# Decoder trunk with stick-breaking attention: another hand-written order for the attention stage and the output projection behind it

## The chip, the cores and the metric

The kernel runs on one core of one Trainium2 chip. The metric is the device time of one execution in microseconds (us); lower is better. The kernel before took 908.56 us (median of three runs, 906.37 to 910.4).

## The reference

The input is one sequence of 512 tokens with 1,024 channels, in fp32. There are two layers, each followed by a squared-ReLU MLP with 4,096 hidden channels, and every sublayer has an RMSNorm before and one behind. The first layer is a pooling mixer. The second is attention with 16 heads of 64 channels; its keys and values come from one projection of the residual stream. What matters here is the second layer's attention, and the projection of its result:

```python
q = jnp.matmul(h, w_q[j])                      # k, v come from w_kv in the same way
z = q_blk @ k_blk.T * inv_sqrt_d               # scores, strictly causal
log1m = jnp.where(mask, -softplus(z), 0.0)
excl = cumsum(log1m, reverse=True) - log1m
a = jnp.where(mask, exp(log_sigmoid(z) + excl), 0.0)
o = a @ v
m = jnp.matmul(o, w_o[j])                      # output projection
x = x + rms_norm(m, mix_post_g)                # norm behind; then a norm ahead of the MLP
```

## The kernel before, in words

**Precision.** Every fp32 product is made of three matmuls: both operands are split into a rounded high part and the rest, the low part, and high times high, high times low and low times high are added up in one PSUM bank. PSUM has 8 banks of 512 columns here, handed out in turn, so a product that needs a bank waits until an earlier one is read.

**Pairs.** Attention goes pair of heads by pair of heads, eight pairs. Of a pair `p` there are, by the letters of the order table:
- `J` and `Q`: the projections of its keys and queries (`project`, `up_block`, L836 to L838, 24 matmuls of 512 columns each). `j` and `q` cast the result out of its bank: ACT writes the high part (L1167, L1168, L1181), DVE the low part (L1170, L1183).
- `S`: the scores, 16 matmuls of up to 512 columns (L1210), into six banks. `G`: ACT's sigmoids, which read them (L1234, L1238).
- `X` and `M`, for each of the two heads: DVE's scan over a row (L1243) and the product with the sigmoid (L1334).
- `T`, for each head: 10 transposes on PE into three banks (L1259) and three copies by ACT (L1261).
- `A`: attention times values, 16 matmuls (L1269); `a`: the split of the result, ACT the high part (L414), DVE the low part (L415).

PE works one pair ahead: between `S` of pair p and `S` of pair p+1 stand `J` and `Q` of p+1, then `A` of p-1 and `T` of p.

**Values.** `V` and `v` are the seven products of the value projection (L1120, 24 matmuls each) and what reads their banks (L1136); `F` makes operands for them. Most lie ahead of the first pair; `V4` and `V6` stand beside pair 0 and pair 1.

**Weights.** Most weights were split earlier in the program and stored in DRAM; SP loads them back as two transfers of 512 KB, high and low (L361, source `kept`), in the order of a queue, each as soon as a slot of its ring is free. The last ones are split during attention itself, in the order of the list `LATE`: the two halves of `V6`'s weight, keys and queries of pairs 4 to 7, the output weights `o0` to `o7` and four weights of the MLP behind. Each goes through `L`, the load of the raw weight by SP (L223; four buffers, `raw` twice, `spare`, `late`); `g`, for keys and queries only, DVE's multiply by the norm's gain (L230); `W`, ACT's cast to the high part (L249; L252 for `V6`); `w`, DVE's subtraction that leaves the low part (L258; L261 for `V6`). `s` stores a split weight to DRAM for later (L203).

SP's queue holds both kinds of loads and takes them one after the other: a load whose buffer is not yet free holds up all loads behind it.

**Output projection.** `Z` is `out_product` for one tile of 128 tokens: `Z034` adds pairs 3 and 4 to tile 0, both halves of 512 columns, three matmuls for each pair and half (L455 to L457). The table does pairs 0 to 6 of tiles 0 and 1; behind the table the last pair follows, and then tiles 2 and 3 whole, half by half. Behind each tile come the squares' sum (L418), the norm of the sum (L507), the norm ahead of the MLP (L532), and the transposes of the normed tile (`transpose`, L541, 8 each), which are read out as `xnh` and `xnl` (L414, L415). The MLP's first products on tiles 0 and 1 need the first two tiles' transposes.

**What sets the order.** In this stage every engine runs its instructions in the order in which the program issues them: PE, ACT, DVE, POOL and SP follow the table `ATT_ORDER` letter by letter, each taking from it what is its own. The loop behind it reads

```python
        with tc.manual_schedule(engines={on.PE, on.Activation, on.DVE, on.Pool, on.SP}):
            for what, i, a in ATT_ORDER:
```

`fill()` in it (behind `J`, `Q`, `V` and the early `W`) issues the next loads of stored weights, as far as the ring has room.

Of the kernel before, what the change touches and what calls it, by code (L numbers as in the profile page):

```python
# [28 lines left out]
PAIRS = HEADS // 2  # L29
# [25 lines left out]
ATT_ORDER = [  # L55
    (w[0], int(w[1:2] or 0), int(w[2:] or 0))
    for w in """V5 N2 v5 V0 N3 V3 F3 v0 J0 v3 F2 j0 Q0 L L L L q0 V1 v1 F1 V2 v2
    S0 G0 X00 M00 J1 W X01 w L V4 M01 j1 T00 T01 W F4 v4 w L Q1 q1 V6 v6 g
    S1 G1 g X10 M10 X11 J2 M11 W j2 w L Q2 W q2 w L A0 a0 T10 T11
    S2 G2 g X20 M20 X21 J3 M21 W j3 w L g Q3 q3 W w L A1 a1 T20 T21  # L60
    S3 G3 g X30 M30 X31 J4 M31 W j4 w L Q4 g q4 A2 a2 T30 T31
    S4 G4 g X40 M40 X41 J5 M41 W j5 w L Q5 W q5 w L A3 a3 T40 T41
    S5 G5 g X50 M50 X51 J6 M51 W j6 w L Q6 W q6 w L A4 a4 T50 T51
    S6 G6 X60 M60 X61 J7 M61 W j7 w L Q7 W q7 w L A5 a5 T60 W w L T61
    S7 A6 G7 X70 Z002 M70 W X71 w Z102 M71 W T70 w R a6 W w L W Z034 Z134 w L W T71 w L Z055 Z155
    W w L A7 W w Z066 Z166 a7 W w s""".split()
]


# [21 lines left out]
def trunk(ctx, tc, x, consts, gcol, grow, pw, wup, wdn, wq, wk, wv, wo, out):  # L91
# [14 lines left out]
    def ps():  # L106
        return psum.tile([P, 512], F32, tag="ps", name=name("ps"))
# [257 lines left out]
    def fill(n=1):  # L365
        if gate[0]:
            behind.update(latest)
        for _ in range(n):
            if queue and sum(map(in_ring, made)) < ahead and (queue[0][0][0] != "dn" or dn_pool[0]):
                if not any(x["key"] == queue[0][0] for x in late) or queue[0][0] in kept:  # L370
                    make()

    def get(key):
        while key not in made:
            make()
        return made.pop(key)
# [68 lines left out]
    def by_twos(w, cut):  # L445

        if len(w.shape) == 3:
            half = w[:, 4 * (cut.start // 512) :][:, : KC // 2]
            return half.rearrange("p (j b) c -> p b c j", j=2)
        half = w[:, NS[cut.start // 512]].rearrange("p (j i) -> p i j", j=2)  # L450
        lo = cut.start % 512 // 2
        return half[:, lo : lo + (cut.stop - cut.start) // 2]

    def mm3(dst, ah, al, bh, bl, start, stop):
        nc.tensor.matmul(dst, ah, bh, start=start, stop=False)  # L455
        nc.tensor.matmul(dst, ah, bl, start=False, stop=False)  # L456
        nc.tensor.matmul(dst, al, bh, start=False, stop=stop)  # L457
# [599 lines left out]
    with tc.tile_pool(name="att", bufs=1, reuse_waits="tile") as ap:  # L1057
# [40 lines left out]
        def value_product(i):  # L1098
            key = VALUES[i][1]
            w = [get(("v", i, h)) for h in range(2)]  # L1100
            banks = [None, None]
            linked = i in (0, 2, 4, 6)
            for t in range(2):
                if key in left:
                    a = [[x[:, q, TS[t]] for q in range(4)] for x in left[key]]
                else:
                    n, k = int(key[0]) - 1, int(key[1]) - 1
                    need(2 * n + t)
                    a = [[x[:, 4 * k + q, TS[2 * n + t]] for q in range(4)] for x in (xnh, xnl)]
                if not linked:  # L1110
                    bank = ps()
                elif i == 0:
                    bank = ps()
                    chain.append(bank)
                else:
                    bank = chain[t]
                for q in range(4):
                    cols = NS[q % 2]
                    for n, (x, z) in enumerate(((0, 0), (0, 1), (1, 0))):
                        nc.tensor.matmul(  # L1120
                            bank, a[x][q], in_turn(w[q // 2][z][:, cols], 512),
                            start=(i == 0 or not linked) and q == 0 and n == 0, stop=q == 3 and n == 2,
                            skip_group_check=True,
                        )

                banks[t] = bank
            fill()
            results[i] = banks
# [155 lines left out]
        def out_product(t, cs, halves=range(2)):  # L1284
            for n in halves:
                if (t, n) not in sums:
                    sums[t, n] = ps()
                for c in cs:
                    if c not in wos:
                        wos[c] = get(("o", c))  # L1290
                    (lh, ll), (wh, wl) = os[c], wos[c]
                    mm3(
                        sums[t, n], lh[:, TS[t]], ll[:, TS[t]], by_twos(wh, NS[n]), by_twos(wl, NS[n]),
                        c == 0, c == PAIRS - 1,
                    )
# [4 lines left out]
        with tc.manual_schedule(engines={on.PE, on.Activation, on.DVE, on.Pool, on.SP}):  # L1300
            for what, i, a in ATT_ORDER:
                if what == "V":
                    value_product(i)
                elif what == "v":
                    value_out(i)
                elif what == "F":
                    form(i)
                elif what == "W":
                    late_high()
                    if upto["W"] < 16:  # L1310
                        fill()
                elif what in "Lgws":
                    {"L": late_load, "g": late_scale, "w": late_low, "s": late_store}[what]()
                elif what == "R":
                    gpost1, gpre1 = gain_row(R_MIX_POST1), gain_row(R_MLP_PRE1, spare_tile())
                elif what == "N":
                    need(i)
                elif what in "JQ":
                    project(("k" if what == "J" else "q", i))
                    fill()  # L1320
                elif what == "j":
                    keys(i)
                elif what == "q":
                    queries(i)
                elif what == "S":
                    pzs[i] = scores((qs[i], ks[i]))
                elif what == "G":
                    for a in range(2):
                        ws[i, a] = sigmoids(pzs[i], a)
                elif what == "X":  # L1330
                    es[i, a] = scanned(a)
                elif what == "M":
                    w = ws[i, a]
                    latest["dve"] = nc.vector.tensor_tensor(out=w, in0=w, in1=es.pop((i, a)), op=ALU.mult)  # L1334
                elif what == "T":
                    parts[i, a] = transposed(ws.pop((i, a)))
                elif what == "A":
                    mix_pair(i)
                elif what == "a":
                    mixed_out(i)  # L1340
                elif what == "Z":
                    out_product(i, range(a // 10, a % 10 + 1))
            assert upto["W"] == upto["w"] == len(late) and not going, upto
            ups = [Update(t, gpost1, None, gpre=gpre1) for t in range(T)]

            def evacuate(t, n):
                up, bank = ups[t], sums.pop((t, n))
                up.halves = (up.halves or []) + [ap.tile([P, 512], F32, tag="at", bufs=6, name=name("at"))]
                up.just_square(n, bank)
                latest["dve"] = nc.vector.tensor_tensor(  # L1350
                    out=up.halves[n], in0=bank, in1=gpost1[:, NS[n]], op=ALU.mult
                )

            for t in range(2):
                for n in range(2):
                    out_product(t, [PAIRS - 1], [n])
                    evacuate(t, n)
                ups[t].factor()
            for t in range(2):
                ups[t].sums_added()  # L1360
                ups[t].rstd()
            for t in range(2):
                ups[t].norm()
            out_product(2, range(PAIRS), [0])
            evacuate(2, 0)
            out_product(2, range(PAIRS), [1])
            ups[0].transpose()
            evacuate(2, 1)
            ups[2].factor()
            out_product(3, range(PAIRS), [0])  # L1370
            ups[2].sums_added()
            ups[1].transpose()
            evacuate(3, 0)
            ups[2].rstd()
            ups[2].norm()
            out_product(3, range(PAIRS), [1])
            fill(4)
            evacuate(3, 1)
            ups[3].factor()
            ups[3].sums_added()  # L1380
            ups[3].rstd()
            ups[3].norm()
            pending.update({t: ups[t] for t in (T - 2, T - 1)})
# [68 lines left out]
```

## Time and profile before

The profiled execution took 908.8 us. Its span, from the first to the last instruction, is 907.0 us, so 1.8 us lie around it. TensorE's granted clock was 0.996 of full speed over the span.

| what | before |
|---|---|
| median of three runs | 908.56 us (906.37 to 910.4) |
| profiled execution, its span | 908.8 us, 907.0 us |
| PE busy | 891.8 us, 98% of the span |
| DVE busy, ACT busy | 700.7 us (77%), 541.2 us (60%) |
| scores of pair 1 (`S1`) start at | 421.23 us |
| first products of the last MLP (L836, 256 columns) start at | 584.02 us |

The trace's lines give the start in us from the span's start, the duration, the engine, the program line, the operation, the tiles written and read, the count, and in brackets the engine's idle time ahead with what ended it. `SPq` is SP's queue of DMA instructions; its duration covers the time for which the instruction was held, not the transfer.

### The profile page before, as it was taken

To read this page: it belongs to the slowest core of one execution; us is meant where nothing else is said; L and a number is where in the kernel's file an instruction comes from. 1 tells how busy PE (TensorE), PEld (TensorE's weight loads), DVE (VectorE), ACT (ScalarE), POOL (GpSimd) and SP (SyncE) were. 2 spreads that over 40 slices of the span, in tenths; PEclk is the share of its full clock that TensorE was granted. 3 is DMA by queue.
4 is the path that set the end of the run, shared out by engine and by line. 5 is a ranking of instruction groups with operands and counts; after the bars stand their busy time and mean duration, and the time that the engine had idled before them with its cause. 6 is when DMAs were issued, how large, how long until landed. Compare 5 with 4: busy or idle time off the path is not lost.

```text
span 907.0 us, 11746 instructions
## 1 busy us (share of the span) xinstructions
PE 891.8 (98%) x4522; PEld 771.0 (85%) x4522; DVE 700.7 (77%) x716; ACT 541.2 (60%) x880; POOL 86.5 (10%) x82
## 2 busy tenths in 40 slices
PE   9999999999999999999999999999999999999997
PEld 7998888888888888878778877898888888888886
DVE  5956799996988976776988884665596876967956
ACT  6757747476796847364778864456554454544632
POOL 2100000000000014000000000111120310403103
PEclk9999999999999999999999999999999999999999
DMA  7443558277696732955121126232504233133102
GB/s 282 172 184 138 177 186 287 114 262 265 241 353 251 268 126 77 383 198 225 47 70 47 47 70 231 79 131 98 205 24 159 96 139 117 47 139 116 45 27 93
DMA packets 39150, 141.01 MB, mean 155 GB/s; under 512 B 3968, under 2 KB 4442, under 8 KB 39094
## 3 DMA queue, kind: packets, MB, share of 16 engines
q1 hardware_dynamic: 38946, 140.24, 42.5%
q8 instruction: 36, 0.59, 0.3%
q14 instruction: 20, 0.16, 0.0%
q10 hardware_dynamic: 148, 0.02, 0.0%
HBM read 116.12 MB, written 24.12 MB: 155 GB/s over the span
## 4 chain that ended last, share of the span: by engine, by line
PE 79%; DVE 7%; ACT 5%; DMA 5%; issue 2%; SPq 0%; POOL 0%; POOLq 0%; DVEq 0%; ACTq 0%
PE ps L723 24%; PE ps L836 13%; PE ps L838 13%; PE ps L837 12%; PE ps L1120 3%; PE ps L455 2%; DMA xn<-in_wdn 2%; PE ps L456 2%; PE ps L457 2%; DMA w<-kept 2%; PE ps L975 2%; PE ps L1210 2%; PE ps L1269 1%; PE ps L951 1%; DMA raw<-in_wup 1%
## 5 line engine op out<-in xcount | busy, mean ns | idle before, releaser
L723 PE MATMUL ps<-w,a 128*128 128x512 f32 x1176 | 267.0, 379 | 0.7 <-ACT a L414 0.7
L836 PE MATMUL ps<-xnh,w 128*128 128x512 f32 (+1 forms) x704 | 254.2, 362 | 2.4 <-DMA w<-kept 2.3
L838 PE MATMUL ps<-xnh,w 128*128 128x512 f32 (+1 forms) x704 | 253.9, 361 | 0.1
L837 PE MATMUL ps<-xnl,w 128*128 128x512 f32 (+1 forms) x704 | 253.8, 361 | 0.0
L723 PEld LDWEIGHTS ps<-w,a 128*128 128x128 f32 x1176 | 221.8, 189 | 33.6 <-ACT a L414 1.5
L836 PEld LDWEIGHTS ps<-xnh,w 128*128 128x128 f32 x704 | 133.2, 190 | 18.0 <-ACT w L252 2.6
L838 PEld LDWEIGHTS ps<-xnh,w 128*128 128x128 f32 x704 | 133.8, 190 | 16.4 <-DMA w<-kept 0.8
L837 PEld LDWEIGHTS ps<-xnl,w 128*128 128x128 f32 x704 | 133.8, 190 | 15.4
L154 DVE TENSOR_TENSOR w<-raw,w 128x1024 fp32r<-128x1024 f32 x56 | 69.3, 1239 | 53.4 <-ACT w L152 53.4
L152 ACT CAST w<-raw 128x1024 fp32r<-128x1024 f32 x56 | 58.5, 1045 | 76.0 <-PE ps L838 75.4
L732 DVE TENSOR_TENSOR y<-ps,y 128x512 f32<-128x512 f32 x124 | 82.7, 682 | 19.6 <-PE ps L723 19.6
L414 ACT CAST w<-e 128x1536 fp32r<-128x1536 f32 (+1 forms) x30 | 41.7, 1391 | 47.3 <-DVE e L696 33.7
L414 ACT CAST a<-r 128x768 fp32r<-128x768 f32 (+1 forms) x60 | 47.0, 785 | 35.3 <-DVE r L677 23.0
L415 DVE TENSOR_TENSOR w<-e,w 128x1536 fp32r<-128x1536 f32 (+1 forms) x30 | 53.9, 1797 | 9.9 <-ACT w L414 9.7
L415 DVE TENSOR_TENSOR a<-r,a 128x768 fp32r<-128x768 f32 (+1 forms) x60 | 60.1, 1002 | 0.6 <-ACT a L414 0.6
L1243 DVE TENSOR_TENSOR_SCAN e<-u,begin 128x1280 f32<-128x1280 f32 x16 | 45.2, 2825 | 17.7 <-ACT u L1234 16.9
L485 POOL TENSOR_TENSOR y<-y,grow 128x512 f32<-128x512 f32 x8 | 12.4, 1546 | 341.8 <-ACT xn L418 341.8
L415 DVE TENSOR_TENSOR w<-xn,w 128x1536 fp32r<-128x1536 f32 (+1 forms) x20 | 33.0, 1651 | 9.4 <-ACT w L414 9.1
L414 ACT CAST w<-xn 128x1536 fp32r<-128x1536 f32 (+1 forms) x20 | 27.8, 1389 | 17.9 <-PE ps L723 17.9
L755 ACT ACTIVATE r<-ps 128x512 f32<-128x512 f32 x56 | 33.0, 590 | 8.6 <-PE ps L838 8.6
L415 DVE TENSOR_TENSOR w<-w,w 128x1536 fp32r<-128x1536 f32 (+1 forms) x20 | 32.9, 1646 | 6.7 <-ACT w L414 6.6
L414 ACT CAST w<-w 128x1536 fp32r<-128x1536 f32 (+1 forms) x20 | 27.9, 1393 | 16.1 <-PE ps L723 15.8
(189 smaller groups left out, 1269.5 us busy)
## 6 DMA issues: line engine op xcount, KB each, us to landing
raw<-in_wup SPq DMA_DIRECT2D x63, 512.0 KB, 4.3
w<-kept SPq DMA_DIRECT2D x42, 512.0 KB, 5.9
w<-in_wdn SPq DMA_DIRECT2D x8, 1536.0 KB, 6.0
xn<-in_wdn SPq DMA_DIRECT2D x8, 1536.0 KB, 8.1
kept<-wx SPq DMA_DIRECT2D x20, 512.0 KB, 5.1
kept<-apart SPq DMA_DIRECT2D x16, 512.0 KB, 6.1
apart<-in_wv SPq DMA_DIRECT2D x10, 512.0 KB, 5.2
raw<-in_wdn SPq DMA_DIRECT2D x8, 512.0 KB, 4.8
```

The costliest lines, as they stand in the source:

```text
L152: nc.scalar.copy(hi, raw)
L154: nc.vector.tensor_tensor(out=lo, in0=raw, in1=hi.bitcast(F32), op=ALU.subtract)
L414: latest["act"] = nc.scalar.copy(hi, src)
L415: latest["dve"] = nc.vector.tensor_tensor(out=lo, in0=src, in1=hi.bitcast(F32), op=ALU.subtract)
L723: nc.tensor.matmul(bank, a[:, x, q, TS[t]], by_twos(w[:, z, q], NS[0]), start=start and q == 0 and k == 0, stop=q == self.n - 1 and k == 2 ...
L732: nc.vector.tensor_tensor(out=part, in0=bank, in1=part, op=ALU.add)
L755: nc.scalar.activation(split_up(r, 256), in_order(pu, 256), ACT.Relu)
L836: nc.tensor.matmul(pu[:, cols], wh[:, k, :], xh, start=k == 0, stop=False)
L837: nc.tensor.matmul(pu[:, cols], wh[:, k, :], xl, start=False, stop=False)
L838: nc.tensor.matmul(pu[:, cols], wl[:, k, :], xh, start=False, stop=k == KC - 1)
L1120: nc.tensor.matmul(bank, a[x][q], in_turn(w[q // 2][z][:, cols], 512), start=(i == 0 or not linked) and q == 0 and n == 0, stop=q == 3 and ...
L1243: nc.vector.tensor_tensor_scan(out=e[:, ::-1], data0=us[a][:, 1:][:, ::-1], data1=begin[:, ::-1], initial=0.0, op0=ALU.mult, op1=ALU.max,)
```

## The change

The table `ATT_ORDER` is rewritten from pair 0 on; `z206` is new, a `Z` for one half only (tile 2, pairs 0 to 6, first half); and the code behind the table puts the transposes of tiles 0 and 1 later. Every engine has as many instructions as before (PE 3114, DVE 678, ACT 735, SP 214 rows of the program, the same kinds).

```diff
@@ ATT_ORDER @@
-    S0 G0 X00 M00 J1 W X01 w L V4 M01 j1 T00 T01 W F4 v4 w L Q1 q1 V6 v6 g
-    S1 G1 g X10 M10 X11 J2 M11 W j2 w L Q2 W q2 w L A0 a0 T10 T11
-    S2 G2 g X20 M20 X21 J3 M21 W j3 w L g Q3 q3 W w L A1 a1 T20 T21
-    S3 G3 g X30 M30 X31 J4 M31 W j4 w L Q4 g q4 A2 a2 T30 T31
-    S4 G4 g X40 M40 X41 J5 M41 W j5 w L Q5 W q5 w L A3 a3 T40 T41
-    S5 G5 g X50 M50 X51 J6 M51 W j6 w L Q6 W q6 w L A4 a4 T50 T51
-    S6 G6 X60 M60 X61 J7 M61 W j7 w L Q7 W q7 w L A5 a5 T60 W w L T61
-    S7 A6 G7 X70 Z002 M70 W X71 w Z102 M71 W T70 w R a6 W w L W Z034 Z134 w L W T71 w L Z055 Z155
-    W w L A7 W w Z066 Z166 a7 W w s""".split()
+    S0 G0 X00 M00 J1 W X01 w V4 M01 j1 T00 T01 W F4 v4 w Q1 q1 V6 v6
+    S1 G1 g g X10 M10 X11 J2 L L M11 W j2 w Q2 q2 A0 a0 T10 T11 W
+    S2 G2 w g X20 M20 X21 J3 M21 W j3 w L L Q3 q3 g A1 a1 T20 T21 W
+    S3 G3 w g X30 M30 X31 J4 M31 W j4 w L L Q4 q4 g A2 a2 T30 T31 W
+    S4 G4 w g X40 M40 X41 J5 M41 W j5 w L L Q5 q5 g A3 a3 T40 T41 W
+    S5 G5 w L L X50 M50 X51 J6 M51 W j6 w L Q6 q6 A4 a4 T50 T51 W
+    S6 G6 w X60 M60 X61 J7 M61 W j7 w L L L Q7 q7 A5 a5 T60 T61 W
+    S7 A6 G7 w L X70 Z002 M70 W X71 w Z102 M71 W T70 w R a6 W w L W Z034 Z134 w L W T71 w L Z055 Z155
+    W w L A7 W w Z066 Z166 z206 a7 W w s""".split()
@@ the loop @@
-                elif what == "Z":
-                    out_product(i, range(a // 10, a % 10 + 1))
+                elif what in "Zz":
+                    out_product(i, range(a // 10, a % 10 + 1), range(2) if what == "Z" else [0])
@@ behind the table @@
-            out_product(2, range(PAIRS), [0])
+            out_product(2, [PAIRS - 1], [0])
             evacuate(2, 0)
             out_product(2, range(PAIRS), [1])
-            ups[0].transpose()
             evacuate(2, 1)
             ups[2].factor()
             out_product(3, range(PAIRS), [0])
             ups[2].sums_added()
-            ups[1].transpose()
+            ups[0].transpose()
             evacuate(3, 0)
             ups[2].rstd()
+            out_product(3, range(PAIRS // 2), [1])
+            ups[1].transpose()
             ups[2].norm()
-            out_product(3, range(PAIRS), [1])
+            out_product(3, range(PAIRS // 2, PAIRS), [1])
             fill(4)
```

**SP's queue around the loads of Q1, J2, Q2, J3 and Q3** (the stored weights, L361, each as high and low) and the raw loads of the late weights (L223):

```order
 L361 DMA w_3353<-kept_1481 128x1024 x2
-L223 DMA raw_3360<-in_wk 128x1024
-L361 DMA w_3386<-kept_2357 128x1024 x2
-L361 DMA w_3438<-kept_2403 128x1024 x2
-L223 DMA raw_3451<-in_wq 128x1024
-L361 DMA w_3478<-kept_2480 128x1024 x2
+L361 DMA w_3384<-kept_2357 128x1024 x2
+L361 DMA w_3436<-kept_2403 128x1024 x2
+L361 DMA w_3474<-kept_2480 128x1024 x2
+L361 DMA w_3506<-kept_2554 128x1024 x2
+L361 DMA w_3584<-kept_2619 128x1024 x2
+L223 DMA raw_3587<-in_wk 128x1024
+L223 DMA raw_3589<-in_wq 128x1024
```

`kept_2357` is Q1's weight. Two raw loads (`k5` and `q5` of `LATE`) stood one ahead of it and one behind the next; now both stand behind five loads of stored weights.

**DVE from the keys of pair 3 to the first scan of pair 3.** Before:

```order
L1170 TENSOR_TENSOR kl_2960<-ps_3736,k_3764 64x512 x2
L258 TENSOR_TENSOR w_3762<-raw_3360,w_3762 128x1024
L230 TENSOR_TENSOR raw_3451<-raw_3451,gc 128x1024
L1183 TENSOR_TENSOR q_3800<-ps_3775,q_3800 64x512 x2
L258 TENSOR_TENSOR w_3805<-raw_3451,w_3805 128x1024
L415 TENSOR_TENSOR ohl_3819<-ps_3810,ohl_3819 128x512
L230 TENSOR_TENSOR spare_3602<-spare_3602,gc 128x1024
L1243 SCALAR_TENSOR_TENSOR e_3902<-u_2963,begin 128x1280
```

and now:

```order
L1170 TENSOR_TENSOR kl_2960<-ps_3732,k_3760 64x512 x2
L258 TENSOR_TENSOR w_3758<-raw_3587,w_3758 128x1024
L1183 TENSOR_TENSOR q_3797<-ps_3772,q_3797 64x512 x2
L230 TENSOR_TENSOR raw_3589<-raw_3589,gc 128x1024
L415 TENSOR_TENSOR ohl_3812<-ps_3803,ohl_3812 128x512
L258 TENSOR_TENSOR w_3853<-raw_3589,w_3853 128x1024
L230 TENSOR_TENSOR spare_3768<-spare_3768,gc 128x1024
L1243 SCALAR_TENSOR_TENSOR e_3898<-u_2963,begin 128x1280
```

The queries' low part (L1183) stands one instruction earlier, ahead of the scaling of the next weight; the second subtraction (L258) stands behind the split of the attention's result. On ACT, at the same place, the cast that this subtraction needs (L249) stood ahead of that split and of the six copies of the transposes; now it stands behind the copies, ahead of the sigmoids of the next pair.

**PE behind the table's last `Z`** (`ohl_4665` is the split result of pair 6, `ohl_4770` before and `ohl_4792` now that of pair 7, `ohl_3641` that of pair 0; `ps_4593` is a sum of tile 0, `ps_4770` now the first half of tile 2). Before, and now:

```order
L457 MATMUL ps_4628<-w_4674,ohl_4665 128x512
L455 MATMUL ps_4593<-h_4754,ohl_4770 128x512
L456 MATMUL ps_4593<-l_4755,ohl_4770 128x512
L457 MATMUL ps_4593<-h_4754,ohl_4770 128x512
L455 MATMUL ps_4603<-h_4754,ohl_4770 128x512
```

```order
L457 MATMUL ps_4628<-w_4674,ohl_4665 128x512
L455 MATMUL ps_4770<-w_4272,ohl_3641 128x512
L456 MATMUL ps_4770<-w_4273,ohl_3641 128x512
L457 MATMUL ps_4770<-w_4272,ohl_3641 128x512
L455 MATMUL ps_4770<-w_4365,ohl_3812 128x512
...
L457 MATMUL ps_4770<-w_4674,ohl_4665 128x512
L455 MATMUL ps_4593<-h_4754,ohl_4792 128x512
```

Between the last matmul on pair 6 and the first on pair 7 now lie the 21 matmuls of `z206`. The transposes of tile 0 (L541) stood behind 48 matmuls of tile 2; now they stand behind the first half of tile 3, and those of tile 1 in the middle of its second half.

More of the change, by code (lines that the diff above doesn't have):

```diff
@@ L57 @@
     for w in """V5 N2 v5 V0 N3 V3 F3 v0 J0 v3 F2 j0 Q0 L L L L q0 V1 v1 F1 V2 v2
-    S0 G0 X00 M00 J1 W X01 w L V4 M01 j1 T00 T01 W F4 v4 w L Q1 q1 V6 v6 g
-    S1 G1 g X10 M10 X11 J2 M11 W j2 w L Q2 W q2 w L A0 a0 T10 T11
-    S2 G2 g X20 M20 X21 J3 M21 W j3 w L g Q3 q3 W w L A1 a1 T20 T21
-    S3 G3 g X30 M30 X31 J4 M31 W j4 w L Q4 g q4 A2 a2 T30 T31
-    S4 G4 g X40 M40 X41 J5 M41 W j5 w L Q5 W q5 w L A3 a3 T40 T41
-    S5 G5 g X50 M50 X51 J6 M51 W j6 w L Q6 W q6 w L A4 a4 T50 T51
-    S6 G6 X60 M60 X61 J7 M61 W j7 w L Q7 W q7 w L A5 a5 T60 W w L T61
-    S7 A6 G7 X70 Z002 M70 W X71 w Z102 M71 W T70 w R a6 W w L W Z034 Z134 w L W T71 w L Z055 Z155
-    W w L A7 W w Z066 Z166 a7 W w s""".split()
+    S0 G0 X00 M00 J1 W X01 w V4 M01 j1 T00 T01 W F4 v4 w Q1 q1 V6 v6
+    S1 G1 g g X10 M10 X11 J2 L L M11 W j2 w Q2 q2 A0 a0 T10 T11 W
+    S2 G2 w g X20 M20 X21 J3 M21 W j3 w L L Q3 q3 g A1 a1 T20 T21 W
+    S3 G3 w g X30 M30 X31 J4 M31 W j4 w L L Q4 q4 g A2 a2 T30 T31 W
+    S4 G4 w g X40 M40 X41 J5 M41 W j5 w L Q5 q5 g A3 a3 T40 T41 W
+    S5 G5 w L L X50 M50 X51 J6 M51 W j6 w L Q6 q6 A4 a4 T50 T51 W
+    S6 G6 w X60 M60 X61 J7 M61 W j7 w L L L Q7 q7 A5 a5 T60 T61 W
+    S7 A6 G7 w L X70 Z002 M70 W X71 w Z102 M71 W T70 w R a6 W w L W Z034 Z134 w L W T71 w L Z055 Z155
+    W w L A7 W w Z066 Z166 z206 a7 W w s""".split()
 ]
```

## The prediction

> **What bounds the kernel now.** First the page's line of busy time, then the table of PE's waits in the stage that is reordered (370 to 600 us), then the timeline around each of them.
>
> ```profile
> PE 891.8 (98%) x4522; PEld 771.0 (85%) x4522; DVE 700.7 (77%) x716; ACT 541.2 (60%) x880; POOL 86.5 (10%) x82
> ```
>
> ```profile
> PE ps L836 <- DMA w<-kept: 2.3, 1, 2.3
> PE ps L1210 <- ACT at L1261: 1.0, 2, 0.8
> PE ps L541 <- DVE xn L532: 0.6, 1, 0.6
> PE ps L1210 <- DVE q L1183: 0.5, 1, 0.5
> PE ps L1210 <- DVE ohl L415: 0.4, 2, 0.2
> PE ps L455 <- ACT ohl L414: 0.4, 1, 0.4
> ```
>
> PE is the bound, and the change leaves its instructions as many as they were. So a gain can only come out of PE's holes: six rows here, 5.2 us together, and what each hole costs behind itself. The largest:
>
> ```profile
> 398.48 0.38 PE L838 MATMUL ps<-xnh,w 128*128 128x512 f32 x1
> ...
> 403.87 2.64 PE L1259 MATMUL ps<-ident,w 128*128 128x128 f32 x20
> 408.86 0.59 PE L836 MATMUL ps<-xnh,w 128*128 128x512 f32 x1 [2.35 <-DMA w<-kept]
> ...
> 410.00 0.80 PE L838 MATMUL ps<-xnh,w 128*128 128x512 f32 x1
> 410.59 0.63 PE L836 MATMUL ps<-xnh,w 128*128 128x512 f32 x1
> 411.02 0.63 PE L837 MATMUL ps<-xnl,w 128*128 128x512 f32 x1
> ...
> 416.05 5.34 PE L1120 MATMUL ps<-w,s 128*128 128x512 f32 x24
> 421.23 0.75 PE L1210 MATMUL ps<-k,q 128*128 128x512 f32 x4
> ```
>
> Q1's 24 matmuls begin at 408.86 and V6 follows at 416.05: 7.19 us. V6's own 24 take 421.23 - 416.05 = 5.18, or 0.216 each, so Q1 lost 2.01 us beside the wait of 2.35. Its rows read 0.63 us, where the row at 398.48 has 0.38, and start 0.43 apart (410.59, 411.02). The clock shows why:
>
> ```profile
> 410.00:420.00 10.00, 10.00 (x41) 8.61 (x42) 5.85 (x8) 1.75 (x3) 0.00 (x0) 0.88 0.27 102
> 470.00:480.00 10.00, 9.21 (x62) 6.90 (x62) 7.71 (x10) 7.44 (x18) 0.00 (x0) 1.00 0.16 54
> ```
>
> The granted clock (third number from the end) is 0.88 behind this hole and 1.00 behind the smaller one at 475.37. The first hole thus costs 2.35 + 2.01 = 4.36 us. What held the weight back stands in SP's queue:
>
> ```profile
> SPq L223 <- DVE w L261: 11.2, 1, 11.2
> ```
>
> ```profile
> 403.28 0.33 SPq L223 DMA_DIRECT2D raw<-in_wk  x1
> 403.72 13.32 SPq L361 DMA_DIRECT2D w<-kept  x4
> ```
>
> The raw load waited 11.2 us for its buffer, until DVE's subtraction for V6 had read it, and Q1's stored weight behind it went out at 403.72 only, to land 5.14 us later.
>
> **Part 1, loads.** In the new queue no raw load stands ahead of Q1's weight. Its slot is that of J1's weight, whose last matmul is the row at 398.48; so the load goes out at about 398.9, 4.8 us sooner. With before's 5.14 us for the high part and 410.00 - 403.72 = 6.28 for the low part, they land at 404.0 and 405.2. PE is done with the transposes at 403.87 + 2.64 = 406.5, so 1.3 us are to spare. Q1 then runs from 406.5 to 411.7, and V6 begins 4.36 us sooner if its own operands are there:
>
> ```profile
> 412.05 1.41 DVE L261 SCALAR_TENSOR_TENSOR w<-raw,gc,w 128x512 fp32r<-128x512 f32 x2
> ```
>
> This row does not hang on Q1: it follows DVE's forms for V6. The weight's second half is complete at 413.46. V6 uses first-half weights for its first six matmuls (411.7 to 413.0), then the second half's high part, and its low part in pieces that end at about 412.8 and 413.5, needed at 413.1 and 413.8. Both bounds: 0 if the pieces are awaited one by one, 413.46 - 411.7 = 1.8 us lost if V6 waits for all of it. I take 0, since the pieces have rows of their own. The stored weight of J2, next in the queue, follows when V4's and Q1's slots come free, by 412.6; S1 now starts at 416.9 and J2 2.3 us behind, at 419.1. The median of these loads says 6.6 us, thus 419.2 at worst:
>
> ```profile
> w<-kept SPq DMA_DIRECT2D x10, 512.0 KB, 6.6
> ```
>
> The two raw loads come behind five stored weights, in the stretch that moves most bytes, and their first user (the scaling behind S2) is 17 us later. **Term: -4.36, bounds -4.4 and -2.5.**
>
> **Part 2, the pairs' order.** S1 to S2 has no hole: 438.35 - 421.23 = 17.12 us, which is PE's pace. From S2 to S7 before:
>
> ```profile
> 438.35 0.82 PE L1210 MATMUL ps<-k,q 128*128 128x512 f32 x4
> ...
> 456.24 0.47 PE L1210 MATMUL ps<-k,q 128*128 128x512 f32 x1 [0.45 <-DVE q L1183]
> ...
> 475.37 1.07 PE L1210 MATMUL ps<-k,q 128*128 128x512 f32 x4 [0.80 <-ACT at L1261]
> ...
> 527.67 0.82 PE L1210 MATMUL ps<-k,q 128*128 128x512 f32 x4
> ```
>
> Five intervals in 89.32 us, 17.86 each: 3.7 us above PE's pace. The change moves ACT's cast `W` from ahead of the transposes' copies to behind them, so the copies free the scores' banks 1.05 us sooner; the holes put down to the copies (L1261) go. But the cast does not vanish: it now stands ahead of the sigmoids, and DVE's scan waits for these. DVE's rows from S2 to S3, then ACT's:
>
> ```profile
> 441.97 2.83 DVE L1243 TENSOR_TENSOR_SCAN e<-u,begin 128x1280 f32<-128x1280 f32 x1 [0.97 <-ACT u L1234]
> ...
> 452.31 1.23 DVE L258 TENSOR_TENSOR w<-raw,w 128x1024 fp32r<-128x1024 f32 x1
> 453.45 1.22 DVE L230 TENSOR_TENSOR raw<-raw,gc 128x1024 f32<-128x1024 f32 x1
> 454.70 1.39 DVE L1183 TENSOR_TENSOR q<-ps,q 64x512 fp32r<-64x512 f32 x2
> ...
> 457.38 0.69 DVE L415 TENSOR_TENSOR ohl<-ps,ohl 128x512 fp32r<-128x512 f32 x1
> ```
>
> ```profile
> 454.70 1.05 ACT L249 CAST w<-raw 128x1024 fp32r<-128x1024 f32 x1 [2.28 <-DVE raw L230]
> 456.26 2.62 ACT L1261 COPY at<-ps 128x512 f32<-128x512 f32 x6
> ```
>
> The loop that closes through DVE: the scan starts 441.97 - 438.35 = 3.62 us behind S, now 1.05 later, 4.67. From the scan to the end of the queries' low part were 456.09 - 441.97 = 14.12 us; the scaling (1.25 by starts) leaves that stretch, 12.87 remain. The next S came 0.15 behind. Sum 17.69, above PE's 17.12: **DVE and ACT become the bound of the pair**, not PE. The scaling, the split of the attention's result (0.69), the subtraction (1.23) and the next scaling now lie between the queries' cast and the scan: 1.22 + 0.69 + 1.23 + 1.22 = 4.36, inside 4.67, so they cost nothing as long as the cast is punctual; without that cover each 0.1 us is 0.1 us per pair. The split stands one scaling later than the queries' cast, and it holds a bank that S needs, as in the two rows of 0.2 us (DVE ohl L415); I allow 0.1 per pair. 17.8 by five gives 89.0. **Term: -0.3, bounds -3.7 (PE's pace) and +4.7** (the scan as late as after S3, worked out under the rivals).
>
> One rule of the Trainium skill bears on these holes. The row at 475.37 shows 0.80 us without work behind 2.4 us of transposes, with no loss of clock; at 408.86 it was 2.35 behind 2.64. The Trainium skill ("TensorE: Matmul & The Clock Gate", Part 1, The HAM clock gate) has the clock halved after a window of about 3.4 us without work, and its Part 4, PE-mode transpose, says that transposes don't count as busy in the same way: 4.99 us against 3.2 us here, which agrees with both rows. By that rule Q1 directly behind its transposes is safe (2.64 us), and so is a pair with a hole under 1.0 us.
>
> **Part 3, the end.** From the last pair's projection on:
>
> ```profile
> 556.10 0.38 PE L457 MATMUL ps<-w,ohl 128*128 128x512 f32 x1
> 556.86 0.48 PE L455 MATMUL ps<-h,ohl 128*128 128x512 f32 x1 [0.38 <-ACT ohl L414]
> 557.63 0.48 PE L456 MATMUL ps<-l,ohl 128*128 128x512 f32 x1 [0.29 <-DVE l L258]
> ...
> 558.55 0.38 PE L455 MATMUL ps<-h,ohl 128*128 128x512 f32 x1
> ...
> 570.64 0.38 PE L457 MATMUL ps<-h,ohl 128*128 128x512 f32 x1
> 571.65 1.29 PE L541 MATMUL ps<-ident,xn 128*128 128x128 f32 x8 [0.64 <-DVE xn L532]
> ```
>
> The fourth matmul on pair 7 starts at 558.55; at 0.216 apart behind the row at 556.10 it would start at 556.96: 1.59 us lost. `z206` now puts 21 x 0.216 = 4.54 us of work there, more than the split of pair 7 and the last output weight are late. The work is only brought forward; the hole goes. The second hole loses 571.65 - (570.64 + 0.22) = 0.79 us: the norm of the first tiles was late. It hangs on the chain of the last store, which does not move against PE, while tile 0's transposes go behind 24 more matmuls (5.2 us), and tile 1's behind 12 more: covered. Late next would be the read-out of tile 1 (xnh, xnl), which the MLP needs 12 matmuls (2.6 us) after its transposes; ACT's and DVE's read-out before took about as long. I allow 0 to 0.2. From S7 to the end of the last `A` the chain of the late weights sets the time, as before; I take 0.1 off, since loads leave sooner. **Term: -2.4, bounds -2.6 and -1.2.**
>
> **Sum.** -4.36 - 0.3 - 2.4 - 0.1 = -7.2 on the profiled execution's 908.8 us: **901.6 us**. The median of the runs, 908.56, stands 0.24 below that execution, inside their spread. A measurement can tell about 0.5% (4.5 us) from no change, so below 904.0 is faster.
>
> **Rivals.**
>
> *Pairs at PE's pace.* If the cast doesn't delay the scan (ACT gets through it while PE still writes the scores), the five intervals take 17.12: 85.6 instead of 89.0. 901.6 - 3.4 = 898.2. For it: the S1-S2 interval. Against: ACT's copies of 2.62 us start near the end of the transposes and leave it no slack.
>
> *The loop turns slower.* At S3 the scan came 4.87 us behind S:
>
> ```profile
> 461.11 2.83 DVE L1243 TENSOR_TENSOR_SCAN e<-u,begin 128x1280 f32<-128x1280 f32 x1 [1.90 <-ACT u L1234]
> ```
>
> If the cast adds its 1.05 to that, the period is 5.92 + 12.87 + 0.15 = 18.94 less the hole of about 0.2 within S, 18.74: five of them 93.7, 906.3, not told from no change. Against: those 4.87 us held the copies that the change frees.
>
> *Q1's gain doesn't come.* If the weight is late for another reason (its slot comes free only behind V4, whose 24 matmuls end where the transposes start, 403.87: the same time as before), Part 1 is zero: 901.6 + 4.4 = 906.0. Against: the loads have slots in turn, and J1's is the next one. V6 awaiting its whole weight is half of this, 903.4.
>
> *Slower: the clock falls in every pair.* If the DVE loop makes PE wait over 1.0 us behind the transposes, half clock follows as at 408.86, 2.01 us each. It decides at a period of 18.1, since 17.12 + 1.0 is the least. Five pairs at 18.1 + 2.0 = 20.1 are 100.6 instead of 89.0: 913.2. For it: the loop is 0.4 from that point. Against: 475.37, with 0.80 and a full clock.
>
> The Trainium skill speaks for this rival beyond the point I set: the same page, A second HAM failure mode: psum-queue depth-cycling, has short idles between groups of matmuls throttle the clock again. In this trace 0.45, 0.80 and 0.64 us did not.
>
> **How the numbers follow.** Forecast (899.5 to 904) 0.53; pairs at PE's pace (897 to 899.5) 0.16; slower loop 0.14; no gain from Q1 or half of it 0.12 (a third of it still below 904); falling clock 0.05. Faster: 0.53 + 0.16 + 0.04, and some of the slower loop's light cases, 0.03, make 0.76. Slower 0.04; the rest, 0.20, is the same. The range leaves out a tenth on each side: 897.5 to 906.5.
>
> **What would show it.** Right: no wait of PE on `w<-kept` near 406, the clock 1.00 in 400 to 420, S1 at 416.9; no ACT L1261 among PE's waits and DVE q L1183 there instead, some 0.5 us in most pairs; S2 to S7 89 us; no wait at L455 to L457 and L541; the first 256-column L836 at 577. Wrong: S1 later than 418.5, S2 to S7 beyond 92, or a clock under 0.95 in a pair.

## The result

The changed kernel takes 899.84 us (median of five runs, 899.55 to 902.47); the kernel before, in the same measurement, 909.6 us (906.37 to 910.4). The ratio is 0.9904, with a 95% interval of 0.9881 to 0.9927: faster by about 1%. A second measurement gave 900.88 against 909.0 us, ratio 0.9897 (0.9874 to 0.9921). The forecast was 901.6 us, with a range of 897.5 to 906.5.

The profiled execution took 899.55 us, its span is 897.8 us. The page's line of busy time, after:

```profile
PE 887.5 (99%) x4522; PEld 771.6 (86%) x4522; DVE 702.7 (78%) x716; ACT 540.6 (60%) x880; POOL 87.1 (10%) x82
```

PE's busy time falls by 4.3 us although it has the same matmuls. Between the scores of pair 0 and those of pair 1 (S0 to S1), where the half clock is gone, it falls from 27.54 to 25.74 us; the rest is spread over the other stages, 1.2 us of it behind the last `A`. Of PE's waits between 370 and 600 us these are left:

```profile
PE ps L1210 <- DVE ohl L415: 1.4, 3, 0.6
PE ps L1120 <- DMA w<-kept: 0.4, 1, 0.4
```

The first hole is gone. The timeline of PE and of SP's queue, after, where Q1 begins, and the two windows whose third number from the end is the granted clock:

```profile
402.50 2.63 PE L1259 MATMUL ps<-ident,w 128*128 128x128 f32 x20
404.89 0.46 PE L836 MATMUL ps<-xnh,w 128*128 128x512 f32 x1
405.19 0.38 PE L837 MATMUL ps<-xnl,w 128*128 128x512 f32 x1
...
415.56 0.75 PE L1210 MATMUL ps<-k,q 128*128 128x512 f32 x4
```

```profile
397.52 0.80 SPq L361 DMA_DIRECT2D w<-kept  x2
...
410.35 6.24 SPq L361 DMA_DIRECT2D w<-kept  x8
416.63 0.57 SPq L223 DMA_DIRECT2D raw<-in_wk  x1
```

```profile
400.00:410.00 10.00, 9.91 (x57) 8.66 (x55) 8.78 (x10) 4.87 (x9) 0.00 (x0) 1.00 0.14 58
410.00:420.00 10.00, 10.00 (x53) 8.54 (x52) 6.64 (x9) 5.50 (x13) 0.00 (x0) 1.00 0.84 298
```

Q1's first matmul has no wait in brackets, SP's raw load comes behind the five stored weights (two loads each), and the clock is 1.00 in both windows (before: 0.95 and 0.88). Q1's weight is the first row of SP's queue: its loads leave at 397.52, as soon as J1's last matmul, at 397.11, is done with the slot.

To compare stages, every profile was cut at the starts of the same matmuls. "J0" is the first matmul of pair 0's keys (about 370 us); ahead of it no experiment changes anything, and yet it starts between 368.2 and 371.7 us in these profiles. So only the lengths between the cuts are compared; "the last A" is the start of the last matmul of pair 7's `A`. All in us:

| kernel | S0 to S1 | S1 to S2 | S2 to S7 | S7 to the last A | from there to the MLP |
|---|---|---|---|---|---|
| before | 30.18 | 17.12 | 89.32 | 25.75 | 30.60 |
| after | 25.89 | 17.12 | 88.76 | 25.57 | 27.96 |
| difference | -4.29 | 0 | -0.56 | -0.18 | -2.64 |
| forecast | -4.36 | 0 | -0.3 | -0.1 | -2.4 |

The stages sum to -7.7 us and the MLP behind takes 0.2 less. The two spans differ by 907.0 - 897.8 = 9.2 us; the rest, some 1.4 us, is the earlier start of J0 (369.71 and 368.26), in code that the change does not touch. For the most part this is also why S1 starts at 415.56 and not at the forecast's 416.9.

In the table as it ran, the row of `S4` has one `L` ahead of `Q5`; the diff in the section on the change prints two.

### The profile page after: what moved, and what is told of

Read it like the earlier page. It is cut to its first block, busy times and chain, and to the rows that moved or that the text cites. A ratio compares the mean times of both kernels' runs of the same rounds, so it can differ in the third digit from the quotient of the medians.

```text
span 897.8 us, 11744 instructions
## 1 busy us (share of the span) xinstructions
PE 887.5 (99%) x4522; PEld 771.6 (86%) x4522; DVE 702.7 (78%) x716; ACT 540.6 (60%) x880; POOL 87.1 (10%) x82
## 4 chain that ended last, share of the span: by engine, by line
PE 93%; DVE 4%; DMA 1%; issue 1%; ACT 0%; SPq 0%; POOL 0%; POOLq 0%; DVEq 0%; ACTq 0%
PE ps L723 28%; PE ps L836 15%; PE ps L838 15%; PE ps L837 15%; PE ps L1120 3%; PE ps L455 3%; PE ps L457 3%; PE ps L456 3%; PE ps L975 2%; PE ps L1210 1%; PE ps L1269 1%; PE ps L1259 1%; DMA w<-kept 1%; PE ps L951 1%; PE ps L541 1%; DVE e L1243 1%
## 5 line engine op out<-in xcount | busy, mean ns | idle before, releaser
L415 DVE TENSOR_TENSOR w<-e,w 128x1536 fp32r<-128x1536 f32 (+1 forms) x30 | 55.1, 1838 | 8.9 <-ACT w L414 8.7
L415 DVE TENSOR_TENSOR a<-r,a 128x768 fp32r<-128x768 f32 (+1 forms) x60 | 60.2, 1003 | 0.6 <-ACT a L414 0.6
L415 DVE TENSOR_TENSOR w<-xn,w 128x1536 fp32r<-128x1536 f32 (+1 forms) x20 | 33.0, 1652 | 9.2 <-ACT w L414 8.9
L415 DVE TENSOR_TENSOR w<-w,w 128x1536 fp32r<-128x1536 f32 (+1 forms) x20 | 34.6, 1728 | 7.0 <-ACT w L414 6.8
```

The source lines that it names most:

```text
L415: latest["dve"] = nc.vector.tensor_tensor(out=lo, in0=src, in1=hi.bitcast(F32), op=ALU.subtract)
```

## The experiments

The lengths of the same stages, for all experiments (the labels are those of the expectations below):

| kernel | median us, before beside it | S0 to S1 | S1 to S2 | S2 to S7 | S7 to last A | to the MLP |
|---|---|---|---|---|---|---|
| only the two loads moved | 904.4, 909.31 | 25.87 | 17.12 | 89.31 | 25.71 | 30.58 |
| after, loads put back | 905.24, 909.31 | 30.01 | 17.11 | 88.76 | 25.21 | 27.96 |
| only the half product | 910.22, 909.31 | 30.50 | 17.11 | 89.32 | 25.89 | 30.92 |
| only the later transposes | 908.27, 909.31 | 31.51 | 17.13 | 89.33 | 25.88 | 29.50 |
| after, old rows of the pairs | 901.12, 908.55 | 25.87 | 17.11 | 89.33 | 25.45 | 27.96 |
| before, transposes ahead of V4 (one run) | 907.03, 908.55 | 28.81 | 17.11 | 89.32 | 26.11 | 30.40 |
| after, scaling on GpSimd | 903.42, 908.55 | 25.88 | 18.40 | 89.39 | 25.75 | 27.96 |
| after, split ahead of scaling | 901.79, 908.55 | 25.88 | 17.11 | 89.54 | 25.67 | 27.96 |
| after, scaling inside the scans | 911.78, 909.0 | 25.88 | 19.97 | 95.29 | 25.39 | 27.96 |
| after, once more | 900.88, 909.0 | 25.88 | 17.11 | 88.75 | 25.44 | 27.96 |
| after, A between the transposes | 899.93, 909.79 | 25.88 | 17.12 | 87.88 | 25.81 | 27.96 |

The pair stage (S2 to S7) repeats within 0.02 us from one execution to the next, so it tells differences that the total cannot. The stage behind it does not: with the same rows it took 25.57, 25.44 and 25.21 us (after, after once more, loads put back).

### The loads alone, and without them

```diff
-    S0 G0 X00 M00 J1 W X01 w L V4 M01 j1 T00 T01 W F4 v4 w L Q1 q1 V6 v6 g
-    S1 G1 g X10 M10 X11 J2 M11 W j2 w L Q2 W q2 w L A0 a0 T10 T11
+    S0 G0 X00 M00 J1 W X01 w V4 M01 j1 T00 T01 W F4 v4 w Q1 q1 V6 v6 g
+    S1 G1 g X10 M10 X11 J2 L L M11 W j2 w L Q2 W q2 w L A0 a0 T10 T11
```

> The kernel before, with only the two raw loads of k5 and q5 moved behind five stored weights in SP's queue. Theory (Q1's weight is held by the raw load ahead of it): no wait on w<-kept near 406, clock 1.00 from 400 to 420, V6 and S1 4.3 us sooner against J1, S2 to S7 89.3 us as before, the end as before; 4.3 us faster in all. Rival (the weight is late for its slot or for the transfers): S1 as before, no gain. Rival (half of it: V6 awaits its own weight): 2.5 us.

The second kernel makes the opposite edit in the changed kernel.

> The changed kernel, with only the two raw loads put back to where they stood before. Theory: the wait of 2.3 us ahead of Q1 and the half clock behind it return, S1 is 4.3 us later against J1, and the rest stays as in the changed kernel; 4.3 us slower than the changed kernel, so about 903 to 905. Rival (the pairs' new order is what freed Q1): no loss.

With the loads alone, S0 to S1 falls from 30.18 to 25.87 us (-4.31), and no other stage moves by more than 0.04. The ratio is 0.9951 (0.9928 to 0.9974). With the loads put back the stage is 30.01, and the two signs of the cause return, here PE's waits and the window of the kernel with the loads back:

```profile
PE ps L836 <- DMA w<-kept: 2.3, 1, 2.3
```

```profile
410.00:420.00 10.00, 10.00 (x41) 8.38 (x41) 6.02 (x8) 1.75 (x3) 0.00 (x0) 0.87 0.26 92
```

So the place of two raw loads in SP's queue makes this term; the rest of the change adds nothing to it. By medians it is worth a little more, 909.31 - 904.4 = 4.9 us. The hole's size varies: in the four executions profiled with both raw loads and transposes as before, the stage took 30.18, 30.01, 30.50 and 31.51, on average 4.7 us above 25.88. The half clock lasted 3.41 us in the first three and 6.83 us in the last.

### The half product alone, and the later transposes alone

The first makes the `z206` edit of the change, with the two code lines that it needs; the second moves the transposes, and leaves `z206` out. The measured stage is the last column.

> The kernel before, with only the half product of the third tile put ahead of the last pair's products. Theory (the norm of tile 0 hangs on the store's transfer, not on PE): the two waits at L455 and L456 go (1.6 us), but PE reaches tile 0's transposes 1.6 us sooner and waits there 2.4 us instead of 0.8: no gain, within 0.3 us. Rival (the terms add): 1.6 us faster, wait at L541 still 0.6.

> The kernel before, with only the transposes of tiles 0 and 1 put later. Theory: the wait of 0.64 us at L541 goes, those at L455 and L456 stay; 0.8 us from pair 7's products to the MLP. Rival (something else holds the MLP's start, the read-out of tile 1): the wait moves to L836, no gain.

The half product alone gains nothing: 30.92 instead of 30.60, ratio 0.9996 (0.9975 to 1.0016). The holes at L455 and L456 are gone, and the one at tile 0's transposes has grown. The timeline of the kernel with only the half product, PE and then ACT:

```profile
568.35 0.38 PE L457 MATMUL ps<-h,ohl 128*128 128x512 f32 x1
571.27 1.29 PE L541 MATMUL ps<-ident,xn 128*128 128x128 f32 x8 [2.55 <-DVE xn L532]
572.32 0.46 PE L455 MATMUL ps<-w,ohl 128*128 128x512 f32 x1
```

```profile
562.25 0.60 ACT L418 ACTIVATE xn<-ps 128x512 f32<-128x512 f32 x1 [4.53 <-PE ps L457]
```

One part of the expectation was wrong: here the norm's chain (its first row is ACT L418) was released by PE's sum, not by the store's transfer. Before, it was the transfer:

```profile
562.63 0.60 ACT L418 ACTIVATE xn<-ps 128x512 f32<-128x512 f32 x1 [4.12 <-DMA kept<-xn]
```

The two come at about the same time: counted from the last matmul of `A`, the norm starts 9.5 us behind it here and 9.2 before. So the half product ahead of the last pair's products cannot bring the norm forward, and the 0.3 us by which it delays the norm are the 0.3 by which the stage is longer.

The later transposes alone gain 30.60 - 29.50 = 1.1 us of this stage (expected 0.8); the waits at L455 and L456 stay, the one at L541 is gone. In total that isn't told apart: 0.9985 (0.9962 to 1.0009). Alone the two edits sum to -0.8 us, together they give -2.64: the half product's gain is collected only where the transposes stand late enough.

### The pairs' rows

The first kernel keeps the new loads and the new end, with the old rows of pairs 1 to 6 (scaling, cast and split). The second puts the split ahead of the scaling in three pairs:

```diff
-    S2 G2 w g X20 M20 X21 J3 M21 W j3 w L L Q3 q3 g A1 a1 T20 T21 W
+    S2 G2 w g X20 M20 X21 J3 M21 W j3 w L L Q3 q3 A1 a1 g T20 T21 W
```

> The changed kernel with the pairs' rows of before (the scaling, the cast and the split where they stood), the moved loads and the new end kept. Theory: S2 to S7 takes 89.3 us again instead of 88.8, everything else as in the changed kernel: 0.6 us slower, about 900.4. Rival (the three parts help each other): more than 1.5 us slower.

> The changed kernel with the split of the attention's result (the letters A, a) ahead of the scaling in pairs 2 to 4. Theory (DVE is full, so what leaves the bank's wait comes back in the scan): the waits on DVE L415 go, but the cast and so the scan come 0.65 us later and PE waits for the queries' low part; S2 to S7 within 0.4 us of 88.8. Rival (only the bank matters): S2 to S7 at 86.4, 2.4 us faster.

The old rows cost 89.33 - 88.76 = 0.57 us, as expected; PE's wait on the copies (L1261, 1.0 us) is back.

With the split first, the waits on DVE L415 go, and S2 to S7 gets longer, 89.54 us (+0.8; expected within 0.4). PE now waits for the queries' low part:

```profile
PE ps L1210 <- DVE q L1183: 1.5, 3, 0.5
```

The scaling (L230) now stands behind the split, so ACT's cast of the scaled weight comes later, and DVE's subtraction (L258) waits for that cast:

```profile
451.71 1.22 DVE L230 TENSOR_TENSOR raw<-raw,gc 128x1024 f32<-128x1024 f32 x1
454.05 1.22 DVE L258 TENSOR_TENSOR w<-raw,w 128x1024 fp32r<-128x1024 f32 x1 [1.12 <-ACT w L249]
```

So the loop of scaling, cast, subtraction and scan has no time to give: what leaves the wait for the bank comes back in it. In the changed kernel, where the bank is awaited, DVE's rows from the queries of pair 3 to the first scan follow one another with one gap of 0.39 us, ahead of the same subtraction:

```profile
448.65 1.39 DVE L1183 TENSOR_TENSOR q<-ps,q 64x512 fp32r<-64x512 f32 x2
450.07 1.23 DVE L230 TENSOR_TENSOR raw<-raw,gc 128x1024 f32<-128x1024 f32 x1
451.33 0.69 DVE L415 TENSOR_TENSOR ohl<-ps,ohl 128x512 fp32r<-128x512 f32 x1
452.41 1.22 DVE L258 TENSOR_TENSOR w<-raw,w 128x1024 fp32r<-128x1024 f32 x1 [0.39 <-ACT w L249]
453.55 1.22 DVE L230 TENSOR_TENSOR spare<-spare,gc 128x1024 f32<-128x1024 f32 x1
454.69 2.82 DVE L1243 TENSOR_TENSOR_SCAN e<-u,begin 128x1280 f32<-128x1280 f32 x1
```

and PE, in the middle of S3, waits for the third of them:

```profile
450.18 0.82 PE L1210 MATMUL ps<-k,q 128*128 128x512 f32 x4
450.93 0.50 PE L1210 MATMUL ps<-kl,q 64*128 64x512 f32 x2
452.07 0.62 PE L1210 MATMUL ps<-kl,q 64*128 64x384 f32 x6 [0.64 <-DVE ohl L415]
```

### Does the clock count transposes as work?

The kernel before, with one letter moved:

```diff
-    S0 G0 X00 M00 J1 W X01 w L V4 M01 j1 T00 T01 W F4 v4 w L Q1 q1 V6 v6 g
+    S0 G0 X00 M00 J1 W X01 w L T00 V4 M01 j1 T01 W F4 v4 w L Q1 q1 V6 v6 g
```

> The kernel before, with the ten transposes of pair 0's first head moved ahead of V4, so that ten and not twenty transposes lie between V4's matmuls and Q1's late weight. Theory 1 (transposes count as idle for the clock): about 3.6 instead of 5.0 us without counted work, as little as the 3.6 us at the end of the run with the half product alone, where the clock stayed at 1.00; so no half clock, Q1 takes 5.2 us from its first matmul, S0 to S1 about 28.2 instead of 30.2. Theory 2 (the empty wait itself counts): the wait is as long as before, 2.3 us, Q1 takes 7.2 us again.

Q1's weight is late as before, its waits are even longer in sum (1.56 + 0.95), and yet the matmuls run at full speed, 0.38 us each. The timeline and the window of this kernel:

```profile
404.12 1.26 PE L1259 MATMUL ps<-ident,w 128*128 128x128 f32 x10
406.94 0.45 PE L836 MATMUL ps<-xnh,w 128*128 128x512 f32 x1 [1.56 <-DMA w<-kept]
407.23 0.38 PE L837 MATMUL ps<-xnl,w 128*128 128x512 f32 x1
408.56 0.48 PE L838 MATMUL ps<-xnh,w 128*128 128x512 f32 x1 [0.95 <-DMA w<-kept]
```

```profile
410.00:415.00 5.00, 5.00 (x25) 4.38 (x24) 2.30 (x5) 1.16 (x2) 0.00 (x0) 1.00 0.08 19
```

Compare the kernel with only the later transposes, whose empty wait was about as long but lay behind twenty transposes:

```profile
406.51 2.64 PE L1259 MATMUL ps<-ident,w 128*128 128x128 f32 x20
410.82 0.53 PE L836 MATMUL ps<-xnh,w 128*128 128x512 f32 x1 [1.67 <-DMA w<-kept]
411.14 0.63 PE L837 MATMUL ps<-xnl,w 128*128 128x512 f32 x1
```

```profile
410.00:415.00 5.00, 3.41 (x8) 2.29 (x9) 3.86 (x5) 2.01 (x3) 0.00 (x0) 0.61 0.27 102
```

From the last matmul to the next, transposes counted as idle, there lie 410.82 - 406.51 = 4.31 us here and 4.99 before, and the clock fell; 406.94 - 404.12 = 2.82 us in this experiment, 3.2 at S4 before, and about 3.75 behind the half product (568.57 to 572.32, with 2.55 us of it an empty wait), and it did not. The empty wait alone does not order these cases: 2.55 without a fall, 1.67 with one. So far theory 1 fits, with a limit between 3.75 and 4.31 us.

Another trace contradicts it. In the kernel with the scaling inside the scans (next section), PE waits 2.27 us behind twenty transposes in three pairs. From the last matmul to the next there lie 5.00, 4.83 and 4.82 us, and the clock fell behind the first of them alone. What orders the cases better is how much PE works in fixed stretches of time. In all these traces the time from one change of the clock to the next is a whole multiple of 3.413 us, and a half clock within the stage lasts one such stretch or two. In stretches counted from where the clock changed (472.93 lies ten of them behind 438.80), the kernel before and then the one with the scaling inside the scans show:

```profile
405.64:409.05 3.41, 0.96 (x7) 0.55 (x6) 2.77 (x3) 3.23 (x7) 0.00 (x0) 1.00 0.83 317
409.05:412.46 3.41, 3.28 (x8) 2.11 (x8) 2.84 (x4) 0.50 (x1) 0.00 (x0) 0.50 0.06 23
```

```profile
435.39:438.80 3.41, 1.63 (x10) 1.18 (x12) 3.33 (x5) 1.09 (x3) 0.00 (x0) 1.00 0.48 154
438.80:442.21 3.41, 3.41 (x15) 2.81 (x12) 1.24 (x2) 3.41 (x10) 1.06 (x1) 0.50 0.50 154
...
472.93:476.35 3.42, 2.20 (x19) 1.78 (x17) 3.34 (x5) 3.38 (x8) 0.00 (x0) 1.00 0.00 0
476.35:479.76 3.41, 2.36 (x15) 1.77 (x16) 2.71 (x4) 1.32 (x3) 0.00 (x0) 1.00 0.48 154
```

The second number of a row is PE's busy time, transposes included. It is 0.96 and 1.63 us in the stretches ahead of the two falls, and 2.20 in the one from 472.93, behind which the clock stayed at 1.00. That one holds transposes alone; the one with 1.63 us holds none. Transposes thus kept the clock up here, and theory 1 is not shown. In the other three falls of this stage PE was busy for 1.05, 1.09 and 1.64 us of the stretch ahead. Of the stretches between 340 and 600 us that were not followed by a fall, the least busy had 1.63 us (behind the half product) and all others 1.8 or more; this experiment's had 1.86. So the order is by busy time, up to a tie at 1.63, and theory 1 and this reading forecast the same for this experiment. No run was made to tell them apart.

The Trainium skill ("TensorE: Matmul & The Clock Gate", Part 1, The HAM clock gate) gives a window of about 3.4 us; the traces agree, with 3.41. Its Part 4, PE-mode transpose, says that transposes do not count as busy in the same way; here a stretch with transposes alone was followed by the full clock, so counting them as idle does not hold in this case.

### Scaling on GpSimd

Since DVE is busy for 78.7 of the 88.8 us from S2 to S7 and GpSimd is idle there, the eight scalings were given to GpSimd (`nc.vector` to `nc.gpsimd` in `late_scale`), first as they stand, then each held by a 128x1 GpSimd instruction that reads what the scan of the pair waits for (the letters `g` then stand behind `G` and behind the first `M`).

> The changed kernel with the eight scalings by the norm's gain (L230) done by GpSimd instead of VectorE. Theory (the split of the attention's result holds a bank only because it stands behind a scaling in DVE's row): the waits of PE on DVE L415 go, S2 to S7 falls from 88.8 to about 86.0, 2.8 us faster than the changed kernel, about 897. Rival (GpSimd is late with the scaling, or slows DVE down): the cast W waits, S2 to S7 at 88.8 or more, no gain.

> The changed kernel with the eight scalings on GpSimd, each held by a small GpSimd instruction until the first or the second scan of its pair begins. Theory (GpSimd's multiply stretches DVE's multiply of two SBUF operands, 2.90 instead of 1.49 us, and leaves the scan alone at 2.82): the products L1334 stay at 1.49 us, the waits on DVE L415 and DVE L1183 go, S2 to S7 takes 86.0 to 86.6 us instead of 88.8, and the kernel is 2.2 to 2.8 us faster than the changed one, about 897.3. Rival (the scan is stretched as well, or GpSimd takes longer than a scan): S2 to S7 at 88 or more, no gain.

Both are slower than the changed kernel, 903.42 and 911.78 us; from S1 to S7 they take 107.8 and 115.3 us, the changed kernel 105.9. The rival held in the first, and the second shows how. DVE's and GpSimd's rows of the second (its lines are numbered two or three higher: L1245 is the scan, L1337 the product with the sigmoid, L232 the scaling; L231 is the added instruction on one column):

```profile
441.05 2.83 DVE L1245 TENSOR_TENSOR_SCAN e<-u,begin 128x1280 f32<-128x1280 f32 x1 [2.17 <-ACT u L1236]
444.00 3.05 DVE L1337 TENSOR_TENSOR w<-w,e 128x1280 f32<-128x1280 f32 x1
```

```profile
441.15 2.70 POOL L231 TENSOR_TENSOR begun<-u,mhalf 128x1 f32<-128x1 f32 x1 [9.57 <-ACT u L1236]
443.81 1.90 POOL L232 TENSOR_TENSOR raw<-raw,gc 128x1024 f32<-128x1024 f32 x1
```

The GpSimd instruction on one column takes 2.70 us, as long as the scan runs (GpSimd's other multiplies of one column, L431, take 0.62 us on average in the kernel before); the scaling starts when the scan ends, and then DVE's product takes 3.05 us where it takes 1.49 alone. The two engines do not share here, they exclude each other: one waits while the other's instruction runs. In pairs 1 to 4 every product meets a scaling, and the period is 2.5 us longer (20.1), and the expectation that the scan leaves GpSimd alone was wrong. The Trainium skill ("SBUF — State Buffer", SBUF: two separate sides) states this: a DVE instruction with two SBUF inputs and a GpSimd instruction that reads SBUF take a shared port pair as an exclusive lock. The trace agrees.

### A between the transposes

```diff
-    S3 G3 w g X30 M30 X31 J4 M31 W j4 w L L Q4 q4 g A2 a2 T30 T31 W
+    S3 G3 w g X30 M30 X31 J4 M31 W j4 w L L Q4 q4 g T30 A2 a2 T31 W
```

and so in pairs 1 to 6.

> The changed kernel with A (attention times values) between the transposes of the two heads, on PE and in the rows of ACT and DVE, in pairs 1 to 6. The bank of A's result is then handed to the sixth bank of the scores and not to an earlier one, needed some 0.4 us later, while DVE's instructions stay the same. Theory (two things bound the pair: that bank, and DVE, which is full): the waits on DVE L415 shrink from 1.4 us to under 0.7, the period goes to DVE's loop of 17.5 to 17.7, S2 to S7 takes 87.8 to 88.3 us instead of 88.8, and the kernel is 0.5 to 1 us faster than the changed one. Rival (only the bank bounds): S2 to S7 at 86.5. Rival (the copies of the transposes wait for A and come late): S2 to S7 at 89 or more.

> The changed kernel once more beside it: 899.8 us, S2 to S7 88.8 us, the same waits on DVE L415 (1.4 us), so that the difference to the run beside it is of one chip.

S2 to S7 takes 87.88 us, 0.9 less than in the changed kernel, with its waits on the split halved:

```profile
PE ps L1210 <- DVE ohl L415: 0.7, 2, 0.5
```

DVE's first scans of pairs 3 and 4 are then 17.72 us apart (those of pairs 2 and 3 17.59), the period of its loop:

```profile
456.53 2.82 DVE L1243 TENSOR_TENSOR_SCAN e<-u,begin 128x1280 f32<-128x1280 f32 x1
...
474.25 2.82 DVE L1243 TENSOR_TENSOR_SCAN e<-u,begin 128x1280 f32<-128x1280 f32 x1
```

The total, 899.93 us (898.79 to 901.13), can't tell this kernel from the changed one (899.84 and 900.88); by its stage it is the better by 0.9 us.

## Why the prediction was right

**What bounds (right).** Only PE's holes could be gained. They were, and the sum of the stages, -7.9 us with the MLP's 0.2, came within a tenth of the forecast's -7.2. The median's gain, 8.1 and 9.8 us in two measurements, is larger. The old hole cost 4.1 to 5.6 us from one execution to the next, where the prediction had only the one profile with 4.36; that may be a part of it, but the executions behind the medians were not profiled.

**Part 1 (right, -4.29 against -4.36).** The raw load at the head of SP's queue was the cause (both edits of the loads), the landed weight left time to spare, and V6 did not await its second half: it starts at 410.30, 0.36 us behind Q1's last matmul. The time to spare was mis-sized: the prediction took 5.14 us from issue to landing and had 1.3 us left, but the loads that left at 397.52 landed in 3.2 us, and Q1 began at 404.89:

```profile
w<-kept SPq DMA_DIRECT2D x2, 512.0 KB, 3.2
```

"Q1's gain doesn't come" is refuted.

**Part 2 (right in sign and size, wrong in where the time goes).** -0.56 against -0.3. The step that failed is "I allow 0.1 per pair" for the bank that the split holds: S3, S4 and S5 lost 0.98, 0.51 and 0.91 us inside the scores (they took 3.30, 2.82 and 3.22 us, where S1, which does not wait, took 2.31). The scaling that the change puts ahead of the split is why: with the split first, these waits are gone. The copies' holes did not go wholly either: pairs 2 and 6 take 0.4 us more than PE's pace, 0.3 of it at the end of the transposes, where the weight load of the scores' matmuls (PEld) waits for the copies:

```profile
PEld ps L1210 <- ACT at L1261: 0.5, 2, 0.3
```

In return PE did not wait for DVE's loop at most of the pairs, as the prediction had it ("DVE q L1183 there instead, some 0.5 us in most pairs": there is no such row). Two errors of opposite sign met, so the closeness of the size is luck. The loop itself was sized well: 17.69 worked out, 17.59 and 17.72 measured once the bank was less in the way, and putting the split first brought the wait on the queries at once. So "DVE and ACT become the bound of the pair" holds, though PE meets that bound in the bank rather than in the queries. "Pairs at PE's pace" (85.6 us) is refuted; "the loop turns slower" too, as 88.8 is far from 93.7. (The term's upper bound, +4.7, is counted from the forecast's 89.0; from the 89.32 of before it would be +4.4.)

**Part 3 (right, -2.64 against -2.4).** No wait at L455 to L457 and at L541 is left. The prediction costed the two holes as two terms; the runs show that they are one: without the later transposes the half product's 1.6 us are waited for again at tile 0's transposes. Its "the chain of the last store" was one of two causes that end together.

**The clock (right for this kernel, but not by its rule).** It stayed at 1.00 in every window of the changed kernel between 400 and 590 us. The rule beside it, that transposes count as idle and that a wait of over 1.0 us behind them therefore halves the clock, did not hold: in the kernel with the scaling inside the scans three pairs had a wait of 2.27 us behind their transposes, and the clock fell in one of them. The forecast did not need the rule, since in the changed kernel PE waits for at most 0.64 us.

**From S7 to the last A:** -0.18 against -0.1. This stage varies by 0.4 us with the same rows, so neither the size nor the reason given ("the chain of the late weights") is shown; after the change PE has no wait in it.

## What to carry to other kernels

A load that waits for its buffer at the head of a queue holds every load behind it; when PE waits for a transfer, look first at when it was issued and at what stood ahead of it there. A hole can cost its own length and then the half clock as well (2.35 and 2.01 us before), and how much PE works in the 3.41 us around it decided that in these runs. So work that is ready belongs next to a load that may be late. Filling a hole gains only if what waits behind the filling is late by less: move both, and test them singly and together.

## What the runs showed of the hardware that was not expected

A GpSimd instruction on one column (128x1) took 2.70 us because it met a DVE scan of 2.83 us, and a DVE product of two SBUF operands took 3.05 instead of 1.49 us when it met a GpSimd multiply of 1.90 us. GpSimd was no free engine in a stage in which DVE worked on SBUF for most of the time. And the clock did not go by the length of a wait: an empty wait of 2.55 us left it at 1.00, one of 1.67 us behind 2.64 us of transposes brought the half clock, and waits of 2.27 us behind twenty transposes did both. It changed in steps of 3.413 us, and a stretch that PE spent on transposes alone (2.20 us of them) was followed by the full clock.
